# Hybrid SSD and attention block: rope's q and k blocks as two pairs in seven products, adaption rows as columns, some of down's weight sums in the z stage

## The chip, the core and the metric

The kernel runs on one core of a Trainium2 chip. A core has five engines with their own instruction streams: TensorE (PE in the profile, its weight loads PEld), VectorE (DVE), ScalarE (ACT), GpSimd (POOL) and SyncE (SP, which here only issues transfers). They meet through semaphores. Data lies in device memory, in SBUF (128 partitions) and in PSUM, where TensorE accumulates. The metric is the device time of one execution in microseconds (us), the median over runs.

## What is computed

One decoder layer over x of 1024 tokens by 1024 channels in float32. A condition c gives six rows of 1024 (shift, scale and gate for two sub-layers): "adaption". Two mixers read the same normalized input, are gated, merged and projected, and a gated convolution FFN follows.

```python
mod = silu(c) @ w_ada + b_ada
sh1, sc1, g1, sh2, sc2, g2 = split(mod, 6)
h = rms_norm(x, pre_norm1_w) * (1 + sc1) + sh1
z, xbc, dt_raw, q, k, v, gates = split(h @ w_in)
y_ssd = ssd_branch(z, xbc, dt_raw, ...)      # conv, SSD in 8 chunks of 128, norm
y_att = diff_attention_branch(q, k, v, ...)  # rope on 16 of 64 dims of each of 16 heads
merged = sigmoid(g_s) * (y_ssd @ w_ssd_o) + sigmoid(g_a) * (y_att @ w_attn_o)
x = x + g1 * rms_norm(merged @ w_out, post_norm1_w)
h2 = rms_norm(x, pre_norm2_w) * (1 + sc2) + sh2
f = (gelu(conv(h2 @ w_up)_gate) * conv(...)_val) @ w_down
x = x + g2 * rms_norm(f, post_norm2_w)
```

Rope turns r1, r2 (the first and second eight of a head's first 16 dims) into r1*cos - r2*sin and r1*sin + r2*cos.

## The kernel before

**Products.** Each float32 operand is split in a high part (`F32R`, made by ScalarE) and the rest, the low part (made by VectorE), and each product of 128x128 with 128x512 becomes three: high*high, high*low, low*high (`mm3`, `block_half`). A block of 128 output channels over all tokens is 8 x 3 products for each half of the tokens, 48 in all. Two blocks taken together as a pair, split in quarters, need seven part products of 4 x 3 in place of eight: 84 in place of 96 (the list `order`, with b11, b21, t2, t1, t3, b22, t4 for the sums of the right side and banks X, Y, Z to collect them).

**Stages**, in order: a head (norm of x, four first blocks, gates 2 and 3); the pairs; z; SSD with the v products as filler; the four rope blocks; the SSD output blocks `so`; attention with the remaining q, k and gate blocks as filler; the attention output; the mix; up in pairs; down in pairs.

**The pairs** (line 292, loop at 703). Eight pairs: four gate blocks, q and k block 2, ten xbc blocks. In product p of pair m, TensorE does 12 products, then the other engines: `x_ahead` splits the weights of three products ahead, `x_sum` makes the weight sums `sab`, ScalarE and VectorE carry the banks to `cgv`, and `post` works on the pair before (tanh for gates, convolution and silu for xbc, split and store for q and k) at the products that `steps_at` names. In pairs 1 and 2 VectorE also adds up adaption.

**Adaption** (`ada_load`, `ada_sum`, `row_load`, `ada_row`). The last four of the six rows are made from 32 tiles of 128 input channels by 1024: each is scaled by its channel's silu(c) and added to `accr` by one scalar_tensor_tensor of 128x1024 (lines 441 and 443). Fourteen fall in pairs 1 and 2, eighteen in z. Where a row is complete (z tiles 2, 7, 14, 22) TensorE sums it over the partitions by two products with `ones` (line 896), VectorE adds the bias and the norm weight on one partition (lines 897 to 901), and it is stored to `rowd`. Rows `rowd[1]` and `rowd[2]` are read back as columns `sh2c`, `a2c`; `rowd[0]` and `rowd[3]` are spread over the partitions as g1r and g2r.

**z** (loop at 906). Three thirds of the width, eight tiles of 128 tokens each, numbered nz. A tile is 24 products of 346 or 348 columns; ScalarE and VectorE make z*(1 + tanh(z/2)) in one of two tiles `ev` (lines 930, 931), which SP stores. In tiles 7 and 15 the next third's weights are split (line 95). Four banks take turns.

**SSD** (loop at 1204). 16 units (chunk, group). `chunk_in` turns x and B by transpositions into a bank px, ScalarE copies it to `xtk`, VectorE makes the masked product `cbm` and `xd` = x*dt (line 1087), GpSimd `xdd` and the skip term in y. `chunk_out` and `chunk_state` follow, between them `fill` emits v products. `down_sums` makes the four weight sums of the later down stage, 44 additions of 128x512 for 11 pairs of blocks, one at each `next(sums_dn)`, four places a unit.

**Rope and so** (loops at 1291 and 1313). q0, k0, q1, k1 hold the 16 rotated dims of all heads. `rope` scales, shuffles partitions on VectorE, multiplies on GpSimd and VectorE, adds, splits; `store_qk` stores 16 pieces of 16 rows a block. Between the blocks `turn_y` transposes the stored y, four token tiles `yr` at a time: the first half in blocks 0 and 1, then `load_y(1)`, the second half in blocks 2 and 3. `fetch_seq` and `split_seq` bring weights two to three blocks ahead. `so` then does eight blocks, both halves of each in turn, with the gate rows `gth` loaded one block ahead.

**What sets the order.** In these stages the order is written out by hand: each engine and SP's queue runs the instructions in the order of the calls (`manual_schedule`). Transfers that stand between the stages are placed by the framework. SBUF tiles of 4 KB a partition come from `Slots`, a list of 43 that is used first in, first out.

Of the kernel before, what the change touches and what calls it, by code (L numbers as in the profile page):

```python
# [14 lines left out]
ALU = mybir.AluOpType  # L15
# [15 lines left out]
NVEC = 269  # L31
# [31 lines left out]
def kernel(ctx: ExitStack, tc: tile.TileContext, a: dict, out: bass.AP, dbg=None):  # L63
# [228 lines left out]
    pairs = [("gs", 4, 5), ("gs", 6, 7), ("qk", 2, 2)] + [("xbc", b, b + 1) for b in range(2, 12, 2)]  # L292
# [25 lines left out]
    qd = [dp.tile([P, S], F32, tag=f"qd{m}", name=f"qd{m}") for m in range(NH)]  # L318
    khd = [dp.tile([64, S], F32, tag=f"khd{m}", name=f"khd{m}") for m in range(NH)]
    kld = [dp.tile([64, S], F32, tag=f"kld{m}", name=f"kld{m}") for m in range(NH)]  # L320
    acd = dp.tile([2 * NH, S], F32, tag="acd", name="acd")
    rowd = [dp.tile([1, D], F32, tag=f"rowd{i}", name=f"rowd{i}") for i in range(4)]
# [7 lines left out]
    def store_qk(kind, b, hi, lo):  # L330
        hi, lo = hi.bitcast(F32), lo.bitcast(F32)
        pieces = []
        if b < 2:
            pieces = [(8 * b + m, 0, 16 * m, 16) for m in range(8)]
        else:
            r = 0
            while r < P:
                m, d0 = divmod((b - 2) * P + r, 48)
                n = min(48 - d0, P - r)
                pieces.append((m, 16 + d0, r, n))  # L340
                r += n
        for m, d0, r, n in pieces:
            if kind == "w_q":
                SP.dma_start(qd[m][d0 : d0 + n, :], hi[r : r + n, :])
                SP.dma_start(qd[m][64 + d0 : 64 + d0 + n, :], lo[r : r + n, :])
            else:
                SP.dma_start(khd[m][d0 : d0 + n, :], hi[r : r + n, :])
                SP.dma_start(kld[m][d0 : d0 + n, :], lo[r : r + n, :])
# [24 lines left out]
    def x_load():  # L373
# [4 lines left out]
        src = {"gs": ("w_gate", "w_gate"), "xbc": ("w_xbc", "w_xbc"), "qk": ("w_q", "w_k")}[kind]["fv".index(n)]  # L378
# [45 lines left out]
    n_ada, n_ald = 0, 0  # L424
    ada_of = {}

    def ada_load():
        nonlocal n_ald
        if n_ald < 32:
            r, k = divmod(n_ald, KD)  # L430
            ada_of[n_ald] = adas[n_ald % len(adas)]
            SP.dma_start(ada_of[n_ald], a["w_ada"][k * P : (k + 1) * P, r * D : (r + 1) * D])
            n_ald += 1

    def ada_sum(load=True):
        nonlocal n_ada
        r, k = divmod(n_ada, KD)
        acc, src = accr[r % 2], ada_of.pop(n_ada)
        n_ada += 1
        if k == 0:  # L440
            V.tensor_scalar(acc, src, scl[:, 0:1], None, op0=ALU.mult)
        else:
            V.scalar_tensor_tensor(acc, src, scl[:, k : k + 1], acc, op0=ALU.mult, op1=ALU.add)
# [6 lines left out]
    u_of = {}  # L450

    def post(m, step):
        kind, *ij = pairs[m] if m >= 0 else ("xbc", 0, 1)
        n = step // 4
# [32 lines left out]
    steps_at = {"gs": {0: (0,), 1: (4,)}, "qk": {0: (0, 1), 2: (4, 5)}, "xbc": {0: (0,), 1: (1,), 2: (2,), 3: (4,), 4: (3, 5), 5: (6,), 6: (7,)}}  # L487
    part = lambda t, k: t[k // 2][:, k % 2, :]
# [13 lines left out]
    with tc.manual_schedule(engines={EN.PE, EN.DVE, EN.Activation, EN.SP}):  # L502
# [89 lines left out]
        for n, (k, half) in enumerate(units):  # L592
# [18 lines left out]
            if n == 11:  # L611
                SL.put(xT.pop(6), crow)
# [59 lines left out]
        HX["t4"] = [new_hl(f"xt4_{k}") for k in range(KH)]  # L672
# [10 lines left out]
        gate_out(pg, 0, gsd[3], vev)  # L683
        for k in range(KH):
# [5 lines left out]
        SL.put(*r22, *r11)  # L690
        evs_x = [SL.get(f"xevs{i}", F32, (P, 2, HALF)) for i in range(2)]
        cgv[0] = [SL.get(f"xc{n}0") for n in "gv"]
        SL.put(vev, *r21, *b12)
        V.tensor_copy(sel, selr)
        accr = [SL.get(f"accr{i}") for i in range(2)]
# [7 lines left out]
        for m, (kind, *_) in enumerate(pairs):  # L703
# [10 lines left out]
            for p in range(7):  # L714
# [31 lines left out]
                for st in steps_at[before].get(p, ()):  # L746
                    post(m - 1, st)
                if m in (1, 2):
                    ada_sum(n_ald < 14)
                    if m == 2 and p == 6:  # L750
                        SL.put(*adas)
                if last:
# [129 lines left out]
    brow, nrow = SL.get("brow"), SL.get("nrow")  # L882
# [1523 lines left out]
```

## Time and profile before

| | us |
|---|---|
| median of 3 runs | 1866.56 (1864.87 to 1866.98) |
| the profiled execution | 1867.69 |
| its span | 1865.8 |
| TensorE busy | 1830.3 |
| VectorE busy | 1311.8 |
| ScalarE busy | 873.2 |
| GpSimd busy | 147.9 |

Times within the profile count from the start of the span. Rows of groups name the line, engine, operation, output and inputs and their shapes, the count, the busy time and the mean of one in ns, and the idle time before them with what ended it. Rows of waits give who waited for whom, the total, the times and the longest. Rows of stretches give from:to, length, then busy time and instructions of PE, PEld, DVE, ACT and POOL, the granted clock of TensorE, the busy share of the DMA engines and GB/s. Timeline rows give start, length, engine, line and operation; equal instructions in a row are merged. Matmuls overlap, so their recorded length is longer than their pace.

### The profile page before, as it was taken

Reading aid. Unit: us, or ns where it says so; the run is one execution under the profiler, and the core shown is the slowest. Engines: PE = TensorE matmul, PEld = TensorE weight load, DVE = VectorE, ACT = ScalarE, POOL = GpSimd, SP = SyncE. Lnnn points to the kernel's source line nnn. Section 1 sums busy time; section 2 is a strip of 40 time slices with the busy share of each in tenths; the row PEclk is TensorE's granted clock in tenths of the full one; section 3 lists DMA queues with packets and bytes.
Section 4 is the critical chain, followed back from the end, with each engine's and each line's share of the span. In section 5 each row is a group of like instructions: output and inputs, shape, how many; then the busy total and the mean of one; then the engine's idle time right before and its main releaser. Section 6 shows DMA issues by size and latency. Waiting matters only on the chain.

```text
span 1865.8 us, 24318 instructions
## 1 busy us (share of the span) xinstructions
PE 1830.3 (98%) x8928; PEld 1524.9 (82%) x8928; DVE 1311.8 (70%) x1962; ACT 873.2 (47%) x1705; POOL 147.9 (8%) x137
## 2 busy tenths in 40 slices
PE   8999999998999999999999999999999999999998
PEld 6788899876788888888887888887788888888886
DVE  7887877799654257767667464487888888876545
ACT  4454532455532135565556232564545454465532
POOL 0000000165411000000000000000000000000001
PEclk9999999999999999999999999999999999999999
DMA  9564366598646746565634655122233322378744
GB/s 363 166 225 170 103 209 227 180 325 306 211 132 180 259 129 175 164 181 143 193 111 136 229 194 185 46 102 102 102 109 111 108 89 104 109 238 304 245 152 159
DMA packets 133382, 325.44 MB, mean 174 GB/s; under 512 B 17392, under 2 KB 41840, under 8 KB 133264
## 3 DMA queue, kind: packets, MB, share of 16 engines
q1 hardware_dynamic: 131952, 320.71, 52.2%
q0 software_dynamic: 1312, 3.19, 0.4%
q8 instruction: 70, 1.15, 0.3%
q14 instruction: 48, 0.39, 0.1%
HBM read 228.54 MB, written 95.31 MB: 174 GB/s over the span
## 4 chain that ended last, share of the span: by engine, by line
PE 74%; DVE 13%; ACT 6%; DMA 4%; issue 3%; POOL 0%; SPq 0%; POOLq 0%; DVEq 0%; ACTq 0%
PE upx L1822 3%; PE upx L1821 3%; PE upx L1823 3%; PE o L1513 3%; PE dx L2185 2%; PE dx L2186 2%; PE dx L2184 2%; PE dy L2184 2%; PE dy L2186 2%; PE dy L2185 2%; PE ao L118 2%; PE so L116 2%; PE so L117 2%; PE ao L117 2%; PE ao L116 2%
## 5 line engine op out<-in xcount | busy, mean ns | idle before, releaser
L1821 PE MATMUL upx<-t,wu_t 128*128 128x512 f32 x264 | 103.6, 392 | 2.3 <-ACT evs L2241 1.5
L1822 PE MATMUL upx<-t,wu_t 128*128 128x512 f32 x264 | 103.0, 390 | 0.2 <-DVE t L1939 0.2
L1823 PE MATMUL upx<-t,wu_t 128*128 128x512 f32 x264 | 102.8, 390 | 0.0
L1795 ACT ACTIVATE wu_t<-sab 128x512 fp32r<-128x512 f32 x57 | 34.1, 627 | 129.8 <-DVE sab L1812 129.8
L1501 ACT COPY aT<-at 128x512 f32<-128x512 f32 (+2 forms) x96 | 46.0, 480 | 103.0 <-PE at L1500 103.0
L95 DVE TENSOR_TENSOR g_lo<-gst,g_hi 128x1024 fp32r<-128x1024 f32 (+1 forms) x42 | 47.5, 1134 | 50.3 <-ACT g_hi L94 50.3
L1513 PEld LDWEIGHTS o<-vt,aT 128*128 128x128 f32 x576 | 74.6, 191 | 9.6 <-ACT aT L1501 5.7
L1513 PE MATMUL o<-vt,aT 128*128 128x128 f32 x576 | 81.0, 277 | 0.2
L94 ACT ACTIVATE g_hi<-gst 128x1024 fp32r<-128x1024 f32 (+1 forms) x42 | 41.4, 988 | 65.2 <-DMA gst<-gld_s 36.6
L1474 DVE TENSOR_REDUCE nmx<-sc 128x1 f32<-128x640 f32 (+3 forms) x64 | 65.6, 1024 | 2.2
L1454 PE MATMUL sc<-kst,qst 128*128 128x512 f32 (+2 forms) x192 | 63.9, 341 | 0.0
L1455 PE MATMUL sc<-klo,qst 128*128 128x512 f32 (+2 forms) x192 | 63.3, 346 | 0.0
L1821 PEld LDWEIGHTS upx<-t,wu_t 128*128 128x128 f32 x264 | 49.6, 188 | 14.6 <-ACT evs L2241 2.0
L1839 DVE SCALAR_TENSOR_TENSOR ug<-cg,vec,ug 128x1023 f32<-128x1023 f32 (+1 forms) x44 | 56.3, 1280 | 6.8 <-ACT ug L1838 5.9
L1822 PEld LDWEIGHTS upx<-t,wu_t 128*128 128x128 f32 x264 | 49.6, 188 | 10.6 <-DVE t L1939 0.5
L1799 DVE TENSOR_TENSOR wu_t<-sab,wu_t 128x512 fp32r<-128x512 f32 x57 | 39.3, 690 | 26.6 <-ACT wu_t L1795 26.6
L1823 PEld LDWEIGHTS upx<-t,wu_t 128*128 128x128 f32 x264 | 49.6, 188 | 10.3
L1839 DVE SCALAR_TENSOR_TENSOR uv<-cv,vec,uv 128x1023 f32<-128x1023 f32 (+1 forms) x44 | 56.2, 1277 | 0.9 <-ACT uv L1838 0.9
L149 POOL TENSOR_TENSOR rsf<-rsf,nhalf 128x1 f32<-128x1 f32 x8 | 5.6, 701 | 627.8 <-DVE rsf L148 625.1
L1490 DVE RECIPROCAL rsm<-ssum 128x2 f32<-128x2 f32 x64 | 10.6, 166 | 63.3 <-ACT p L1487 36.2
L1500 PE MATMUL at<-ident,p 128*128 128x128 f32 x288 | 47.8, 275 | 6.4 <-DVE p L1492 4.9
L1492 DVE SCALAR_TENSOR_TENSOR p<-p,coef,p 128x128 f32<-128x128 f32 (+3 forms) x64 | 52.4, 818 | 2.3
(550 smaller groups left out, 5921.1 us busy)
## 6 DMA issues: line engine op xcount, KB each, us to landing
adas<-in_w_ada SPq DMA_DIRECT2D x32, 512.0 KB, 5.1
wdr<-in_w_down SPq DMA_DIRECT2D x22, 512.0 KB, 6.6
wtd<-wds SPq DMA_DIRECT2D x22, 512.0 KB, 4.8
wuf<-in_w_up SPq DMA_DIRECT2D x22, 512.0 KB, 3.4
gld_s<-gsum SPq DMA_DIRECT2D x22, 512.0 KB, 2.8
gst<-gld_s SPq DMA_DIRECT2D x20, 512.0 KB, 4.4
wdt_raw<-wtd SPq DMA_DIRECT2D x20, 512.0 KB, 4.8
wuv<-in_w_up SPq DMA_DIRECT2D x19, 512.0 KB, 3.5
```

The source lines that it names most:

```text
L116: T.matmul(ps, lh, rh, start=(i == 0), stop=False)
L117: T.matmul(ps, lh, rl, start=False, stop=False)
L1454: T.matmul(sc[:, n0:n1], qs_[s][:, tsl], ks_[s][:, n0:n1], start=True, stop=False)
L1474: V.reduce_max(nmx[:, bq, s : s + 1], sc[:, :L], axis=AX.X, negate=True)
L1513: T.matmul(po_of[j, grp][:, qi, :], at[:, k, :], vt[j % 2][:, kt, :], start=(kt == 0), stop=(kt == i))
L1821: T.matmul(out_, wh, xh_, start=(k == 0 and first), stop=False, skip_group_check=not first)
L1822: T.matmul(out_, wh, xl_, start=False, stop=False, skip_group_check=not first)
L1823: T.matmul(out_, wl, xh_, start=False, stop=(k == end), skip_group_check=not first)
L1839: V.scalar_tensor_tensor(u[:, d:], c_[:, : S - d], fw[:, 2 - d : 3 - d], u[:, d:], op0=ALU.mult, op1=ALU.add)
L2184: T.matmul(o, gh[:, kk, tsl], wh, start=(k == 0 and not more), stop=False, skip_group_check=more)
L2185: T.matmul(o, gh[:, kk, tsl], wl, start=False, stop=False, skip_group_check=more)
L2186: T.matmul(o, gl[:, kk, tsl], wh, start=False, stop=(k == KF - 1), skip_group_check=more)
```

## The change

- **Rope.** q0 with k0 and q1 with k1 become pairs 3 and 4 of the pairs stage (ten pairs now). The order of the rotated dims within a block is changed, so that partners lie 64 partitions apart; two transfers within SBUF exchange the halves into `sw`, and VectorE multiplies, adds and splits in steps named by `steps_at["rope"]`, the last one in the pair after. q, and k's high and low parts, lie in device memory as one array each, so that a block of 16 dims is stored by one transfer for each part.
- **Before so.** Only w_q block 3 is left there (taken from attention's filler). Its two halves carry the first four and the next four transpositions of y; then come half 0 of so 0, four transpositions of the second half, half 0 of so 1, the other four, and then the second halves. Attention's first filler is 8 units in place of 20.
- **Adaption.** The weights lie transposed; each tile of 128 outputs by 1024 inputs is multiplied with the row `crow` and summed to one column of `adac`, the bias as start (`dot`, line 183). `ada_end`, in z tile 22, makes all columns, transposes two groups on TensorE and stores two rows; `sh2c` and `a2c` are columns of `adac`.
- **Down's sums.** Loads begin in z tile 8, and tiles 10 to 21 take one sum each; SSD units have three places in place of four.
- **SSD.** `xd` reads the bank px in place of `xtk`.
- Some tiles change places in `Slots`: `crow` is kept to the end of z, r11 is freed before the tiles of t4 are taken, b12 earlier.

```diff
-    pairs = [("gs", 4, 5), ("gs", 6, 7), ("qk", 2, 2)] + [("xbc", b, b + 1) for b in range(2, 12, 2)]
+    pairs = [("gs", 4, 5), ("gs", 6, 7), ("qk", 2, 2), ("rope", 0, 0), ("rope", 1, 1)] + [("xbc", b, b + 1) for b in range(2, 12, 2)]
...
         if b < 2:
-            pieces = [(8 * b + m, 0, 16 * m, 16) for m in range(8)]
+            for src, dst, d0 in ((hi, qd, 0), (lo, qd, 64)) if kind == "w_q" else ((hi, khd, 0), (lo, kld, 0)):
+                SP.dma_start(dst[b, d0 : d0 + 16, :, :].rearrange("d h s -> (d h) s"), src)
+            return
...
-        if k == 0:
-            V.tensor_scalar(acc, src, scl[:, 0:1], None, op0=ALU.mult)
-        else:
-            V.scalar_tensor_tensor(acc, src, scl[:, k : k + 1], acc, op0=ALU.mult, op1=ALU.add)
+        dot(adac[:, n_ada : n_ada + 1], src, crow, src, vec[:, V_BA + n_ada : V_BA + n_ada + 1])
...
+        elif kind == "rope":
+            w_, d = ("w_q", "w_k")[n], step % 5
+            sw = swt[n]
+            if d == 0:
+                SP.dma_start(sw[:64, :], c_[64:, :])
+                SP.dma_start(sw[64:, :], c_[:64, :])
+            elif d == 1:
+                V.scalar_tensor_tensor(c_, c_, qscale[w_], rop[0], op0=ALU.mult, op1=ALU.mult)
+            elif d == 2:
+                V.scalar_tensor_tensor(sw, sw, qscale[w_], rop[1], op0=ALU.mult, op1=ALU.mult)
+            elif d == 3:
+                V.tensor_tensor(c_, c_, sw, op=ALU.add)
+                A.activation(sw.bitcast(F32R), c_, AF.Copy)
+            else:
+                V.tensor_tensor(c_.bitcast(F32R), c_, sw, op=ALU.subtract)
+                store_qk(w_, b, sw, c_)
...
+    steps_at["rope"] = {0: (0,), 1: (5,), 2: (1,), 3: (2, 6), 4: (3,), 5: (7, 4), 6: (8,)}
...
+                if m > 1 and pairs[m - 2][0] == "rope" and p == 0:
+                    post(m - 2, 9)
...
-    def ada_row(r):
...
-        for half in range(2):
...
-            T.matmul(pr, ones, acc[:, hsl], start=True, stop=True)
-            V.tensor_tensor(br[:, hsl], pr[0:1, :], br[:, hsl], op=ALU.add)
...
+    def ada_end():
...
+        V.scalar_tensor_tensor(a2c, a2c, 1.0, vcol(V_PN2), op0=ALU.add, op1=ALU.mult)
+        V.scalar_tensor_tensor(gcol[:, :KD], adac[:, :KD], 0.5, vcol(V_PO1), op0=ALU.mult, op1=ALU.mult)
+        V.tensor_tensor(gcol[:, KD:], adac[:, 3 * KD :], vcol(V_PO2), op=ALU.mult)
...
+        T.transpose(pr[: 2 * KD, :P], gcol, ident)
+        V.tensor_copy(growt[: 2 * KD, :], pr[: 2 * KD, :P])
...
-                if nz in (2, 7, 14, 22):
-                    ada_row((2, 7, 14, 22).index(nz))
+                if nz == 22:
+                    ada_end()
+                if nz == 8:
...
+                    sums_dn = all_sums()
+                    down_load(0)
+                    down_load(1)
+                elif 10 <= nz < 22:
+                    next(sums_dn)
...
-        V.tensor_tensor(v3(xd[:, gs]), v3(xtk[:, gs]), bc64(dt[:, c, hs]), op=ALU.mult)
+        V.tensor_tensor(v3(xd[:, gs]), v3(px), bc64(dt[:, c, hs]), op=ALU.mult)
...
-            next(sums_dn, None)
             if u % 2 == 1:
                 chunk_norm(u // 2)
...
-    seq = [("w_q", 0), ("w_k", 0), ("w_q", 1), ("w_k", 1)] + [("w_ssd_o", j) for j in range(8)]
+    seq = [("w_q", 3)] + [("w_ssd_o", j) for j in range(8)]
...
+        for half in range(2):
+            block_half(ps[:, half, :], seq_w[0], hT, half)
+            for k in range(4 * half, 4 * half + 4):
+                turn_y(k, 0)
+            if half == 0:
+                split_seq(1)
+        load_y(1)
...
+        store_qk("w_q", 3, hi, lo)
...
+        def so_half(j, half):
+            if half == 0:
+                pso[j] = ps_mm(f"so{j}")
+                fetch_seq(j + 3)
+                SP.dma_start(gths[j % 2], gsd[j])
+            block_half(pso[j][:, half, :], seq_w[j + 1], yT, half)
+            if half == 0:
+                split_seq(j + 2)
...
+            V.scalar_tensor_tensor(mout[:, hsl], gth[:, hsl], 1.0, pso[j][:, half, :], op0=ALU.add, op1=ALU.mult)
...
+        so_half(0, 0)
+        for k in range(4):
+            turn_y(k, 1)
+        so_half(1, 0)
+        for k in range(4, 8):
+            turn_y(k, 1)
...
+        so_half(0, 1)
+        so_half(1, 1)
...
-    NFIRST, NLAST = 20, 20
+    NFIRST, NLAST = 8, 20
```

More of the change, by code (lines that the diff above doesn't have):

```diff
@@ L683 @@
         gate_out(pg, 0, gsd[3], vev)
+        SL.put(*r11)
+        HX["t4"] = [new_hl(f"xt4_{k}") for k in range(KH)]
         for k in range(KH):
@@ L959 @@
     assert n_ada == 32
-    SL.put(*ev, zraw, *cgv[1], *adas, *accr, brow, nrow)
+    SL.put(*ev, zraw, *adas, crow)
     singles.close()
@@ L1268 @@
     hi, lo = [SL.get(f"th{n}", F32R) for n in ("hi", "lo")]
-    qf = SL.get("qf")
-    sw = SL.get("sw")
-    perm = [(i + 8) % 16 + 16 * (i // 16) for i in range(32)]
     def split_seq(n):
```

179 lines of the change are left out of this document (65 added, 114 removed).

## The prediction

> **What bounds the kernel.** I read the page's busy shares first, then the busy time by stretches cut at the stage borders, then TensorE's waits.
>
> ```profile
> span 1865.8 us, 24318 instructions
> PE 1830.3 (98%) x8928; PEld 1524.9 (82%) x8928; DVE 1311.8 (70%) x1962; ACT 873.2 (47%) x1705; POOL 147.9 (8%) x137
> core 0: us, PE busy (x) PEld busy (x) DVE busy (x) ACT busy (x) POOL busy (x), PEclk, DMA share, GB/s
> 94.30:248.10 153.80, 153.04 (x674) 126.01 (x673) 128.15 (x164) 78.48 (x119) 1.18 (x2) 1.00 0.51 171
> 248.10:349.40 101.30, 99.65 (x606) 95.35 (x605) 67.48 (x109) 26.48 (x48) 4.41 (x9) 1.00 0.67 215
> 349.40:518.80 169.40, 162.65 (x842) 128.26 (x841) 143.51 (x196) 93.00 (x249) 87.50 (x63) 1.00 0.75 261
> 518.80:569.60 50.80, 50.80 (x257) 42.74 (x256) 29.81 (x36) 20.38 (x30) 11.33 (x5) 1.00 0.44 123
> 569.60:656.60 87.00, 87.00 (x385) 72.10 (x384) 26.06 (x33) 11.71 (x13) 3.43 (x1) 1.00 0.73 228
> ```
>
> The stretches are: pairs in seven products, z, SSD with v, the four rope blocks, the SSD output blocks (so). TensorE is never without work for long, at granted clock 1.00. So a product taken away counts in full, unless something then comes late, and the question is where the wait moves. The so stretch gives the pace: 384 products of 128x512 in 87.0 us, 0.2266 us each. The waits that TensorE has in these stretches:
>
> ```profile
> PE pst L1133 <- DVE tt L1116: 5.6, 4, 2.5
> PE z L117 <- DVE wz_lo L95: 1.7, 1, 1.7
> ```
>
> **1. Rope's blocks as two pairs.** Four blocks of 48 products, 192, become two pairs of 7 x 12, 168: 24 x 0.2266 = **-5.4 us**. w_q 3 only changes stage: its 48 products (10.9 us) leave attention's filler and enter before so.
>
> The pairs bring their rotation into the stage. In one pair VectorE does 7 splits, 4 sums and 3 evictions (all 128x512, 14 in all) and for rope 4 scalar_tensor_tensor and 4 additions or subtractions of 128x1024:
>
> ```profile
> L395 DVE TENSOR_TENSOR xw_t<-xsab,xw_t 128x512 fp32r<-128x512 f32 x24 | 16.6, 690 | 10.5 <-ACT xw_t L394 10.5
> L478 DVE SCALAR_TENSOR_TENSOR xbcT<-xcv,vec,xbcT 128x1023 f32<-128x1023 f32 (+2 forms) x18 | 23.0, 1279 | 1.3 <-ACT xbcT L475 1.1
> L1284 DVE TENSOR_TENSOR qf<-qf,sw 128x1024 f32<-128x1024 f32 x4 | 4.9, 1226 | 9.1 <-POOL qf L1282 9.1
> 190.00:209.00 19.00, 19.00 (x85) 15.73 (x85) 16.07 (x21) 10.17 (x15) 0.00 (x0) 1.00 0.36 112
> ```
>
> 14 x 0.69 + 4 x 1.28 + 4 x 1.23 = 19.7 us recorded, in a pair of 84 x 0.2266 = 19.0; instructions overlap by some 0.08 each, so 17.9 is needed: VectorE is 94% full, where an xbc pair shows 16.07 of 19. The lag grows through two pairs. ScalarE's copy that makes q's high half waits for VectorE's addition, and behind that copy are queued the next weight split and the copy of bank X, which product 2 of the next pair needs. Following both queues by these durations, TensorE waits 0.2 us at the second rope pair and 1.4 at the pair behind it, where ScalarE's convolution start comes on top. I take **+1.5**, bounds 0 (products are split three ahead) and 4 (the lag in every pair left). The exchange of halves is a transfer on SP's queue that is read two to three products (5.4 to 8.2 us) later. In all, 16 transfers of the rotation (8 exchanges, 8 stores) replace 64 stores on that queue. The second pair's exchange must wait until the first pair's store has read the same tile, and behind it on SP stand the next weight loads; those have four products (10.9 us) before a sum reads them. I price SP at nothing in this stage; without that cover it would be a few us, and the bound of 4 holds it.
>
> **2. Adaption rows.** The products with ones go:
>
> ```profile
> 259.54 0.33 PE L118 MATMUL z<-wz_hi,hT 128*128 128x346 f32 x1
> 259.70 1.88 PE L896 MATMUL adar<-accr,ones 128*128 128x512 f32 x4
> ...
> 261.58 0.32 PE L117 MATMUL z<-wz_lo,hT 128*128 128x346 f32 x1
> ```
>
> Without a row L117 would follow at 259.86; it comes at 261.58, so a row costs 1.72 and four cost 6.9. But a row also covered VectorE at the end of a third of z, where the next third's low weights are split:
>
> ```profile
> 280.38 2.45 DVE L95 TENSOR_TENSOR wz_lo<-wz_raw,wz_hi 128x692 fp32r<-128x692 f32 x3
> 280.43 1.88 PE L896 MATMUL adar<-accr,ones 128*128 128x512 f32 x4
> 313.32 1.27 DVE L897 TENSOR_TENSOR brow<-adar,brow 1x512 f32<-1x512 f32 x2
> 314.62 1.21 DVE L899 SCALAR_TENSOR_TENSOR brow<-brow,nrow 1x1024 f32<-1x1024 f32 x1
> 315.76 2.45 DVE L95 TENSOR_TENSOR wz_lo<-wz_raw,wz_hi 128x696 fp32r<-128x696 f32 x3
> ```
>
> At the first border the first low part is ready 0.82 after 280.38, at 281.2. Without the row TensorE wants it at 280.6: a new wait of 0.7. At the second border L897 and L899 go (2.4 us of VectorE), a down sum of 0.6 comes in, and TensorE is itself 1.72 earlier: the wait of 1.7 stays. Last, the new transposition behind tile 22 stands in TensorE's queue and waits for a VectorE chain behind that tile's own eviction:
>
> ```profile
> L930 ACT ACTIVATE ev<-z 128x330 f32<-128x330 f32 (+2 forms) x24 | 10.9, 454 | 69.2 <-PE z L118 44.7 <-DVE sm L926 24.5
> L931 DVE SCALAR_TENSOR_TENSOR ev<-ev,z 128x330 f32<-128x330 f32 (+2 forms) x24 | 12.2, 507 | 23.8 <-ACT ev L930 21.5 <-DMA zd<-ev 2.4
> L203 DVE TENSOR_TENSOR a<-a,vec 128x1 f32<-128x1 f32 x8 | 1.3, 159 | 0.3
> ```
>
> 0.45 + 0.51 + 3 x 0.16 and a transposition of 0.1 make 1.5 us; the old row found its sums long done. In all -6.9 + 0.8 + 1.5 = **-4.6**, bounds -8.6 (no wait left) and -2. The multiply-and-sum has the form of line 184, below, against the scalar_tensor_tensor of the same width (1279 above). So it is the same VectorE time, beside products; its loads keep their count and size, and the small loads of rows on POOL's queue and of two columns on SP's go at no gain, since nothing waited for them.
>
> ```profile
> L184 DVE CUSTOM_DVE_ANT_0 ada0a<-ada0a,crow,vec 128x1024 f32<-128x1024 f32 x3 | 3.8, 1277 | 0.0
> ```
>
> **3. Down's sums and SSD.** 12 of 44 sums move to z, and xd reads PSUM:
>
> ```profile
> L783 DVE TENSOR_TENSOR wds<-wdr,wds 128x512 f32<-128x512 f32 x11 | 13.4, 1219 | 0.4
> L786 DVE TENSOR_TENSOR wds<-wdr,wdr 128x512 f32<-128x512 f32 x11 | 8.7, 793 | 0.0
> L1087 DVE TENSOR_TENSOR xd<-xtk,sm 128x512 f32<-128x512 f32 x16 | 14.8, 924 | 0.0
> L1116 DVE TENSOR_TENSOR tt<-po,sm 128x512 f32<-128x512 f32 x14 | 9.5, 680 | 0.0
> ```
>
> These sums cost 0.79 to 1.22 here, about 1.0, so 12 us leave SSD. xd takes the form of tt: 16 x (0.924 - 0.680) = 3.9 us less. xd starts no earlier, since the masked product before it on VectorE still follows ScalarE. VectorE falls from 143.5 to some 127 of 169. TensorE's wait in SSD (5.6) is for tt, so for its lag; total idle is 169.4 - 162.65 = 6.75. I take **-4.5**, bounds 0 and -6.7: one of four slots per unit goes, the lag shrinks but the burst before tt stays.
>
> **4. Before so.** This order has less cover. The second half of y may load only after the first half's last transposition, and its own transpositions now come after one half block (24 x 0.2266 = 5.4 us), where before two half blocks and more lay between:
>
> ```profile
> 537.62 1.47 PE L1263 MATMUL ytr<-ident,yr 128*128 128x128 f32 x12
> L1169 SPq DMA_DIRECT2D yr<-yd x4: 319/377/1027, 538.8 to 540.8; - x4
> DMA to landing us min/median/max: 6.8/6.8/6.8
> 543.08 0.42 SPq L344 DMA_DIRECT2D qd<-thhi  x1
> gth<-gsd SPq DMA_DIRECT2D x8, 512.0 KB, 5.7
> ```
>
> The transpositions end at 539.1 (537.62 + 1.47), the fourth load is issued at 540.8 and lands 6.8 later, at 547.6: 8.5 us. So TensorE waits 8.5 - 5.4 = 3.1. Behind the loads SP holds 8 stores of w_q 3 (which wait for VectorE), one weight block and then the gate rows: issued some 9 us after those transpositions (VectorE's low half done at 5.7, then eight issues of 0.42), 5.7 to landing, so at 14.5. VectorE's first product with the gate waits for them, and the second four transpositions need the banks that VectorE frees behind it: 1.4 more. **+4.5**, bounds 1 and 9.
>
> **5. The rest.** Attention starts with 2 filler units in place of 14 (8.2 us less cover for its first loads, which are issued before so ends): +0.5, bounds 0 and 2. The transfers added to z are taken at +0.5, bounds 0 and 3 (rival C).
>
> **Sum.** -5.4 - 4.6 - 4.5 + 1.5 + 4.5 + 0.5 + 0.5 = -7.5 us. The profiled execution took 1867.7 (span 1865.8 and 1.9 around it), 1.1 above the median of 1866.6: 1860.2 for such an execution, **1859 us** for the median.
>
> **Rivals.** A: the load before so takes its upper bound, 9 us in place of 4.5. For it: SP's queue and the bank chain hold each other. Against it: the loads are first in line. 1859 + 4.5 = 1864.
> B: SSD's lag is not made by the moved sums, so that part does nothing: 1859 + 4.5 = 1863.5. For it: the sums before tt stay. Against it: the wait is for tt, which stands behind two sums in VectorE's order.
> C, the slower side: z runs out of transfers.
>
> ```profile
> 286.00:346.00 60.00, 58.35 (x359) 56.00 (x358) 38.59 (x68) 12.43 (x25) 2.42 (x5) 1.00 0.71 225
> 410.00:425.00 15.00, 14.89 (x79) 11.52 (x78) 14.48 (x19) 8.21 (x21) 8.88 (x7) 1.00 1.00 366
> ```
>
> 60 us move 13.5 MB; five loads of 1 MB and three stores of 1 MB, less the three loads of 0.5 MB already there, add 6.9: 20.4 MB want 340 GB/s. SSD shows that 366 is possible. If z gets 275, its transfers need 74 us; 14 late, in front of VectorE's in-order queue and of SSD's first weights: 1859 + 14 = 1873. It decides above some 8 us of lateness, at 300 GB/s. [...]
> D: the wait before so throttles TensorE.
>
> ```profile
> 20.00:24.00 4.00, 3.33 (x11) 1.72 (x10) 2.73 (x8) 1.75 (x5) 1.02 (x1) 0.72 1.03 422
> 432.00:436.00 4.00, 1.58 (x7) 0.94 (x6) 3.96 (x6) 0.59 (x1) 0.30 (x1) 1.00 0.94 359
> ```
>
> In the head, after gaps, the granted clock fell to 0.72 over 4 us, a loss of 0.28 x 4 = 1.1 us; 2.4 us without a product at 432 left it at 1.00. With 3.1 in one piece it may fall: 1860. [...]
> E: the new waits of 1, 2 and 4 are half what I take, and SSD gives all of its 6.7: about 1853.
>
> **Chances.** Forecast (1855 to 1862.5) 0.54; A 0.11; B 0.08; C 0.11; D 0.07; E 0.09. About 0.2% (3.7 us) is what a measurement of this kernel can tell from no change. Faster: the forecast, D and E, 0.70; within it A and B, 0.19; slower C, 0.11. The range 1851 to 1868 leaves out C and the edge of E.
>
> **What would show it.** The pairs stretch has 840 products and about 192 us; rows of line 896 are gone; TensorE waits for the transposition behind z's tile 22 and for the low weights at the first border; SSD is shorter by 4 to 5 us with "pst from tt" small; before so TensorE waits for the load of y some 3 us; one product stage of 48 and 384 of so with 64 transpositions take about 105 us and those waits. It is wrong if the pairs wait in every pair, if z's low weights or v's come late for transfers, or if y's load lands 12 us after its transpositions.

## The result and the profile after

The changed kernel takes 1909.62 us (median of 4 runs, 1906.27 to 1914.37) against 1866.57 for the kernel before: a ratio of 1.0234, 95% interval 1.0211 to 1.0258. It is slower by 43 us, where 7.5 us of gain were forecast. Its profiled execution took 1906.27, with a span of 1904.5.

The stretches of the changed kernel, cut at the same stage borders as in the prediction (from:to, length, busy time of PE, PEld, DVE, ACT and POOL with instructions, granted clock, DMA share, GB/s): pairs, z, SSD, then w_q 3 with so, and then, counted again from the same start, everything up to the first block of the attention output.

```profile
94.10:296.50 202.40, 192.58 (x841) 157.12 (x840) 164.76 (x222) 94.94 (x145) 0.00 (x0) 1.00 0.53 177
296.50:402.50 106.00, 96.30 (x598) 94.95 (x597) 67.13 (x131) 25.35 (x46) 1.04 (x1) 0.97 0.75 258
402.50:568.40 165.90, 161.73 (x834) 127.62 (x833) 122.29 (x182) 92.97 (x248) 79.60 (x62) 1.00 0.63 223
568.40:708.80 140.40, 115.17 (x507) 93.93 (x506) 37.47 (x53) 24.12 (x38) 0.92 (x2) 0.93 0.47 159
568.40:1080.20 511.80, 480.86 (x2626) 404.63 (x2624) 292.74 (x578) 244.06 (x624) 17.05 (x18) 0.98 0.53 158
```

The last line answers to this stretch of the kernel before:

```profile
518.80:1042.00 523.20, 516.08 (x2818) 436.51 (x2817) 316.03 (x603) 253.91 (x637) 31.27 (x22) 1.00 0.56 166
```

Four blocks of 48 products have left that stretch, 192 x 0.2266 = 43.5 us. So 479.7 was to be had, and with the forecast waits of 5 us 484.7; it took 511.8. That is the largest miss, 27.1 us. TensorE is idle for 511.80 - 480.86 = 31 us there, and the granted clock fell to 0.98 in the mean, 0.93 up to 708.80. The second is z, 106.0 where 96.7 + 0.5 was forecast. The third is the pairs: two more pairs, 168 products or 38.1 us, should have made 153.8 into 191.9 and a wait of 1.5; they take 202.4. SSD is 3.5 us shorter, about as forecast. Behind attention both kernels take the same, 823.8 and 824.3.

TensorE's waits in the changed kernel show the three places:

```profile
PE so L117 <- DVE mout L1319: 21.3, 5, 8.4
PE xx L416 <- ACT xevs L741: 5.9, 3, 3.0
PE z L117 <- ACT wz_hi L95: 5.4, 1, 5.4
PE ytr L1275 <- DMA yr<-yd: 3.9, 3, 2.0
PE xx L416 <- DVE xcv L755: 2.8, 3, 2.0
PE z L118 <- DVE wz_lo L96: 2.3, 2, 1.5
PE adat L913 <- DVE gcol L911: 2.0, 1, 2.0
```

### so: the gate rows

In the groups of VectorE, the product with the gate idles for a transfer (first row). In the kernel before (second row) it had 50.9 us of idle time, all for TensorE's products:

```profile
L1319 DVE SCALAR_TENSOR_TENSOR mout<-gth,so 128x512 f32<-128x512 f32 x16 | 11.0, 687 | 92.0 <-DMA gth<-gsd 46.9 <-PE so L119 45.1
L1329 DVE SCALAR_TENSOR_TENSOR mout<-gth,so 128x512 f32<-128x512 f32 x16 | 10.3, 684 | 50.9 <-PE so L118 50.9
```

The timeline of one border between blocks, first SP's queue, then VectorE and TensorE:

```profile
643.57 0.32 SPq L1321 DMA_DIRECT2D msd<-mout  x1
643.94 0.42 SPq L1258 DMA_DIRECT2D qst<-qd  x1
644.41 1.44 SPq L1261 DMA_DIRECT2D kst<-khd  x2
645.89 1.23 SPq L1261 DMA_DIRECT2D klo<-kld  x2
647.22 0.53 SPq L1199 DMA_DIRECT2D w_ssd_o_raw<-in_w_ssd_o  x1
647.80 0.43 SPq L1313 DMA_DIRECT2D gth<-gsd  x1
655.51 0.69 DVE L1319 SCALAR_TENSOR_TENSOR mout<-gth,so 128x512 f32<-128x512 f32 x1 [10.84 <-DMA gth<-gsd]
656.25 0.79 PE L117 MATMUL so<-yT,w_ssd_o_hi 128*128 128x512 f32 x1 [8.00 <-DVE mout L1319]
```

The store of a block's result waits until the block is done. Behind it on SP's queue stand attention's first loads (behind blocks 3 and 4), a weight block, and then the gate row that the running block needs at its middle. It is issued at 647.80 and there at 655.5; TensorE's second half waits 8.0 us for VectorE's product with it. Without attention's loads in front (blocks 2 and 3) the same wait is 2.5 and 2.3 us. A block now loads its own gate row, where the kernel before loaded the next block's. There attention's first loads also stood behind the gate row on the queue, and not ahead of it.

### z: a store behind loads

```profile
337.70 2.81 SPq L800 DMA_DIRECT2D wdr<-in_w_down  x4
340.60 2.10 SPq L358 DMA_DIRECT2D wz_raw<-in_w_zdt  x3
342.80 0.42 SPq L358 DMA_DIRECT2D zraw<-in_w_zdt  x1
343.48 0.79 SPq L946 DMA_DIRECT2D zd<-ev  x1
352.01 0.52 DVE L945 SCALAR_TENSOR_TENSOR ev<-ev,z 128x346 f32<-128x346 f32 x1 [7.61 <-DMA zd<-ev]
362.54 0.31 ACT L877 ACTIVATE sm<-sm 128x128 f32<-128x128 f32 x1 [6.03 <-DVE sm L876]
363.59 2.11 ACT L95 ACTIVATE wz_hi<-wz_raw 128x696 fp32r<-128x696 f32 x3
364.41 0.66 PE L117 MATMUL z<-wz_hi,hT 128*128 128x348 f32 x1 [5.39 <-ACT wz_hi L95]
```

Down's four loads of 512 KB and the four loads of the next third's weights are issued just ahead of a store of z. Only two tiles `ev` take turns, so VectorE waits 7.61 us until that store has read its tile. All that stands behind on VectorE and ScalarE is late by it: ScalarE waits for `sm`, and behind that stand the weight splits of the last third. TensorE waits 5.39 us for them and starts again at half its pace: up to 369.94 the granted clock is 0.50 and the products start 0.29 us apart, from 370.20 on it is 1.00 and they start 0.16 apart. While the burst runs, the DMA engines are busy all the time (0.96 and 1.03 in the column before the last), though z as a whole shows 0.75:

```profile
340.00:345.00 5.00, 5.00 (x34) 5.00 (x33) 4.23 (x12) 0.69 (x3) 0.00 (x0) 1.00 0.96 351
345.00:350.00 5.00, 5.00 (x33) 5.00 (x32) 0.00 (x0) 0.46 (x1) 0.00 (x0) 1.00 1.03 372
```

### Pairs: the exchange

```profile
201.03 0.33 SPq L335 DMA_DIRECT2D kld<-xcv  x1
201.63 1.20 SPq L377 DMA_DIRECT2D xwv<-in_w_xbc  x1
202.94 0.47 SPq L462 DMA_DIRECT2D sw<-xcv  x1
209.71 1.23 DVE L465 SCALAR_TENSOR_TENSOR xcv<-xcv,ropc 128x1024 f32<-128x1024 f32 x1 [2.64 <-DMA sw<-xcv]
213.33 0.50 PE L416 MATMUL xx<-xt,xw_t 128*128 128x512 f32 x1 [1.96 <-DVE xcv L755]
222.99 1.24 ACT L489 ACTIVATE xbcT<-xcg,vec 128x1024 f32<-128x1024 f32 x1
224.13 0.57 ACT L741 COPY xevs<-xx 128x512 f32<-128x512 f32 x1
224.76 0.50 PE L416 MATMUL xx<-xt,xw_t 128*128 128x512 f32 x1 [2.98 <-ACT xevs L741]
```

The second rope pair's exchange for k stands on SP behind the first pair's last store, which waits for VectorE, and a weight load. Its first half is issued at 202.94, and at 209.71 VectorE, which multiplies in place, has waited 2.64 us for it. The lag comes out at TensorE as 1.96 us in that pair and 2.98 in the next.

### The profile page after: what moved, and what is told of

The parts are those of the page before. It is cut to its first block, busy times and chain, and to the rows that moved or that the text cites. A ratio compares the mean times of both kernels' runs of the same rounds, so it can differ in the third digit from the quotient of the medians.

```text
span 1904.5 us, 24191 instructions
## 1 busy us (share of the span) xinstructions
PE 1831.0 (96%) x8889; PEld 1522.7 (80%) x8889; DVE 1303.8 (68%) x2004; ACT 878.7 (46%) x1717; POOL 121.3 (6%) x122
## 4 chain that ended last, share of the span: by engine, by line
PE 67%; DVE 14%; DMA 9%; ACT 5%; issue 2%; SPq 1%; POOL 0%; DVEq 0%; POOLq 0%; ACTq 0%
PE upx L1822 3%; PE upx L1823 3%; PE upx L1824 3%; PE o L1518 3%; PE at L1505 2%; PE dx L2186 2%; PE ao L118 2%; PE ao L119 2%; PE ao L117 2%; PE dx L2187 2%; PE upy L1822 2%; PE dx L2185 1%; PE upy L1823 1%; PE upy L1824 1%; PE sc L1460 1%
## 5 line engine op out<-in xcount | busy, mean ns | idle before, releaser
L1518 PEld LDWEIGHTS o<-vt,aT 128*128 128x128 f32 x576 | 74.8, 191 | 10.1 <-ACT aT L1506 6.0
L1319 DVE SCALAR_TENSOR_TENSOR mout<-gth,so 128x512 f32<-128x512 f32 x16 | 11.0, 687 | 92.0 <-DMA gth<-gsd 46.9
L117 PE MATMUL so<-yT,w_ssd_o_hi 128*128 128x512 f32 x128 | 52.9, 413 | 21.3 <-DVE mout L1319 21.3
L416 PE MATMUL xx<-xt,xw_t 128*128 128x512 f32 x120 | 47.6, 396 | 9.8 <-ACT xevs L741 5.9
```

The lines of the kernel that those rows point to most:

```text
L117: T.matmul(ps, lh, rh, start=(i == 0), stop=False)
L416: T.matmul(o, wh, xh_, start=(k == 0 and first), stop=False, skip_group_check=not first)
L1518: T.matmul(po_of[j, grp][:, qi, :], at[:, k, :], vt[j % 2][:, kt, :], start=(kt == 0), stop=(kt == i))
```

## The experiments

All are the changed kernel with one edit, unless the text says otherwise. "Stage" means here the stretch from the last v product to the attention output (511.8 us in the changed kernel).

### Gate rows one block ahead

```diff
+        for n in range(2):
+            SP.dma_start(gths[n], gsd[n])            # ahead of the w_q 3 block
...
-                SP.dma_start(gths[j % 2], gsd[j])
+                if 2 <= j < 7:
+                    SP.dma_start(gths[(j + 1) % 2], gsd[j + 1])
...
         so_half(0, 1)
+        SP.dma_start(gths[0], gsd[2])
         so_half(1, 1)
```

> The changed kernel, with the gate rows of a block loaded one block ahead again (rows 0 and 1 ahead of the second half of y, row j+1 at the start of block j), as the kernel before did. Theory G, that the late gate rows carry the loss in so: VectorE's idle time for the gate rows falls from 46.9 us to under 10, TensorE's wait for the product with the gate from 21.3 to under 5, and the time by 18 to 24 us, to 1886 to 1892. Rival Y, that the reload of y and the lower clock behind it carry the loss: the gate rows only take a wait that another one replaces, and the time falls by under 8 us, to 1902 or more.

Measured: 1883.11 us, 26.5 less than the changed kernel (1.0089 of before, 1.0074 to 1.0105). VectorE's group and TensorE's waits between 610 and 670 us of this kernel:

```profile
L1322 DVE SCALAR_TENSOR_TENSOR mout<-gth,so 128x512 f32<-128x512 f32 x16 | 11.0, 687 | 62.3 <-PE so L119 62.3
PE so L117 <- DVE mout L1322: 3.9, 5, 0.8
```

No idle time for gate rows is left, and the stage takes 489.1. Theory G holds, and gives some 2 us more than it asked for; rival Y is out as the main cause. Two things remain: five waits of 0.78, and the reload of y.

### Both products with the gate behind the second half

```diff
-            V.scalar_tensor_tensor(mout[:, hsl], gth[:, hsl], 1.0, pso[j][:, half, :], op0=ALU.add, op1=ALU.mult)
             if half == 1:
+                for h_ in range(2):
+                    hsl = slice(h_ * HALF, (h_ + 1) * HALF)
+                    V.scalar_tensor_tensor(mout[:, hsl], gth[:, hsl], 1.0, pso[j][:, h_, :], op0=ALU.add, op1=ALU.mult)
                 SP.dma_start(msd[j], mout)
```

This is on top of the gate rows one block ahead.

> The changed kernel with the gate rows one block ahead and both products with the gate of a block behind the block's second half, as the kernel before had them, where the changed kernel puts the first product between the halves. With the gate rows alone five or six blocks show a wait of TensorE of 0.78 us at the second half for the first half's product (3.9 us in all; six stretches of 10 us show 9.22 busy). If the order makes it (the second half writes the same tile that the product reads): these waits go, and the time falls by 4 to 5 us, to 1878 to 1879. If VectorE is late for another reason, the wait moves to the next block's first half: within 1.5 us of 1883.

Measured: 1878.75, 4.4 us less than with the gate rows alone; the stage 483.7 in place of 489.1, and the row "so from mout" is gone from TensorE's waits. The changed kernel asks VectorE to read one half of a two-half PSUM tile while TensorE is to write the other; the program makes TensorE wait until that read is done (0.78 us a time: the 0.69 of the product and its way). That wait was hidden under the late gate rows.

### A second set of tiles for y

```diff
+        ysets.append([SL.get(f"yr{i}") for i in range(4, 8)])
+        load_y(1)                                     # at the start of the w_q 3 block
...
-        load_y(1)
```

Two kernels have it: the changed kernel with this edit alone, and the one with the gate rows one block ahead.

> The changed kernel, with a second set of four tiles for y, so that the second half of y is loaded at the start of the w_q 3 block and not behind the first half's last transposition; the gate rows still come when the changed kernel loads them. If the waits add up: TensorE's gap of some 5.4 us at the second half's transpositions goes and the clock behind it stays at 1.00, so the time falls by 6 to 8 us, to 1902 to 1904. If the gate rows are the later of the two anyway, they take the wait's place: under 3 us.

Measured: 1909.13, the same as the changed kernel (1909.62). TensorE no longer waits for y's load, but 2.8 us for VectorE at the same transpositions, and its wait for the gate product is 22.9 us in place of 21.3: the gate rows were the later of the two.

> The changed kernel with the gate rows one block ahead and a second set of tiles for y. With the gate rows alone it took 1883.1, and from the end of v to the first output block of attention 489.1 us, with 3.17 us of 588 to 593 without a product and the granted clock at 0.92 and 0.74 there (4.5 and some 1.7 us lost). If the reload of y and the clock behind it are hidden by the second set: 5 to 7 us less, 1876 to 1878, and the clock 1.00 throughout so. If something else holds the second half's transpositions (the banks, VectorE): less than 2 us.

Measured: 1880.23, 2.9 us less than with the gate rows alone (1883.11), where 5 to 7 were expected; the stage falls from 489.1 to 483.7, by 5.4. The granted clock is 1.00 in the whole stage. The stage shows the expected size; the whole time shows less. In its profiled execution z and SSD, which this edit does not touch, are longer (z 106.6 in place of 105.8, SSD 167.0 in place of 166.2).

### Down's sums in SSD again

```diff
-                if nz == 8:
-                    ...
-                    down_load(0)
-                    down_load(1)
-                elif 10 <= nz < 22:
-                    next(sums_dn)
...
             run_bg(1)
+            next(sums_dn, None)                       # fourth place of an SSD unit
```

> The changed kernel, with all of down's weight sums in SSD again and none in z. Theory Z, that the loads of down's weights stand ahead of z's stores: VectorE's wait for the stores of z (14.3 us) falls to about 2.4 as before, TensorE's wait for the high weights (5.4) goes, z takes 97 to 99 us in place of 105.7; SSD takes 0 to 4 us more, since 12 sums of about 1 us return to a VectorE with slack. Time 4 to 8 us lower. Rival: the multiply-and-sum columns and the new transposition make z's waits; then z stays over 103 us, and the time is the same or up to 4 us higher.

Measured: 1898.87, 10.7 us less. z takes 95.9 in place of 106.0, and SSD 167.2 in place of 165.9. Theory Z holds, its size was set too low. It also prices two parts of the change apart: the adaption columns bring z from 101.3 to 95.9, 5.4 us; the moved sums gain 1.3 in SSD and cost 10.1 in z.

### Four tiles for z's stores

```diff
-    ev = [SL.get(f"ev{i}", F32, (P, 2, HALF)) for i in range(2)]
+    ev = [SL.get(f"ev{i}", F32, (P, 2, HALF)) for i in range(4)]
```

> The changed kernel with four tiles for what z stores in place of two; down's sums and their loads stay in z, and nothing else moves. Theory Z, that only the turn of two store tiles passes the late transfer on to VectorE, ScalarE and TensorE: VectorE's wait for z's stores (14.3 us) falls under 3, TensorE's wait for the high weights (5.4) under 1, z falls from 106.0 to 97 to 99 us, and the time by 6 to 9 us. Rival C, that z has more to move than its transfers manage: the late transfer then shows at the weights of z or at the adaption's loads, z stays over 102 us, and the time falls by less than 4.

Measured: 1904.49, 5.1 us less. z itself follows theory Z. This kernel's stretches z and the first 23 us of SSD, TensorE's wait at the start of SSD, and the issue of v's first weights on SP's queue:

```profile
295.50:391.90 96.40, 94.16 (x597) 92.94 (x595) 65.88 (x129) 24.18 (x44) 1.04 (x1) 1.00 0.78 273
391.90:415.00 23.10, 16.94 (x80) 13.49 (x80) 13.94 (x25) 14.24 (x36) 4.28 (x4) 0.85 0.52 179
PE v L1056 <- ACT wv_hi L1034: 6.2, 1, 6.2
393.45 1.45 SPq L1025 DMA_DIRECT2D wv_raw<-in_w_v  x3
```

z falls to 96.4, so the two store tiles were what passed the lateness on. But SSD rises from 165.9 to 171.9: now v's first weights are late, a wait of 6.2 us, with a clock of 0.85 over the 23 us. The eight loads of v's weights take 5.0 us in the median from issue to landing (5.7 in the changed kernel). But the first of them are issued only behind the last store of z, at 393.45, where the changed kernel issues the first one at 377.38, 25 us before z ends. So this wait comes from the time of their issue and not from slow transfers. Why this kernel places them so late, and whether z would still be short with them further ahead, no run shows.

### The exchange on POOL's queue

```diff
-                SP.dma_start(sw[:64, :], c_[64:, :])
-                SP.dma_start(sw[64:, :], c_[:64, :])
+                G.dma_start(sw[:64, :], c_[64:, :])
+                G.dma_start(sw[64:, :], c_[:64, :])
...
-            sw = swt[n]
+            sw = swt[2 * b + n]
```

> The changed kernel, with the exchange of halves of the two rope pairs issued on POOL's queue, which is empty in that stage, and into tiles of its own for each pair. Theory S, that the exchange comes late on SP's queue: VectorE's wait of 2.6 us for the exchange goes, TensorE's waits at the second rope pair and the two behind it (2.5 + 3.0 + 0.6 us) fall to 1.5 to 3, and the time falls by 3 to 4.5 us. Rival V, that VectorE is simply full there (94% by my own sum): the waits move by less than 1 us and the time by less than 1.5.

Measured: 1905.87, 3.7 us less; the pairs take 199.6 in place of 202.4, and VectorE no longer waits for the exchange. The pairs stretch of kernels in which nothing of it was changed went from 201.1 to 204.0, so a gain of 3 is about what can be told here. Theory S is supported, and half of the waits stay. The edit gives the exchange another queue and tiles of its own at once; which of the two frees it, this run does not tell.

### A tile that is still being stored

```diff
-        SL.put(vev, *r21)
+        SL.put(*r21, vev)
```

> The changed kernel with one line of the list of free tiles turned round, so that the first convolution's output in the pairs stage doesn't get the tile of which the last gate block is still being stored. TensorE's wait in the first pair falls from 2.4 us to 0.5 as in the kernel before; time 2 us lower, which the runs can hardly tell. If it stays 2.4, ScalarE waits for something else there.

TensorE's waits in the first pair (94 to 113 us) of this kernel; in the changed kernel the same row has 2.4, since ScalarE's convolution start waits 1.8 us for a store of the last gate block to leave its tile:

```profile
PE xx L416 <- ACT xevs L741: 0.5, 1, 0.5
```

The pairs take 200.8 in place of 202.4, the time is 1905.24; the difference of 4.4 to 1909.62 is more than the row explains, and within the spread of the changed kernel's own runs.

### All of it together

Gate rows ahead, products with the gate behind the second half, a second set for y, down's sums in SSD, the exchange on POOL's queue, the tile handed out last.

> The changed kernel with all of it together: gate rows one block ahead, both products with the gate behind the second half, a second set of tiles for y, down's sums in SSD again, the exchange of halves on POOL's queue with tiles of its own per pair, and the slot of the last gate tile of the first stage handed out last (that one should take the wait of 2.4 us at the first pair). If the effects add up: 1909.6 - 26.5 - 10.7 - 3.7 - 4.5 - 6 - 2 = 1856, range 1853 to 1860, faster than the kernel before (1867). If the rope pairs keep a lag of VectorE's own, or a new wait comes up: 1861 to 1867.

Measured: 1858.27 (1857.15 to 1859.49), 0.9955 of before (0.9940 to 0.9970). The single gains add up to 26.5 + 4.4 + 2.9 + 10.7 + 3.7 + 4.4 = 52.6, which would give 1857.0. The changed kernel's loss is accounted for as a whole; the smaller gains in this sum are within the spread of the runs, so it does not confirm them one by one. Its stretches are pairs, z, SSD and the stage:

```profile
93.80:291.80 198.00, 193.29 (x842) 158.27 (x841) 164.82 (x222) 94.77 (x145) 4.27 (x8) 0.99 0.55 182
291.80:387.70 95.90, 94.20 (x598) 93.23 (x597) 61.25 (x121) 26.98 (x50) 2.08 (x2) 1.00 0.68 226
387.70:554.90 167.20, 162.85 (x833) 128.23 (x833) 132.70 (x193) 90.97 (x245) 81.47 (x61) 0.99 0.72 257
554.90:1033.00 478.10, 472.45 (x2625) 400.18 (x2624) 292.49 (x578) 243.41 (x624) 17.03 (x18) 1.00 0.57 169
```

### Columns and xd alone

The kernel before with the adaption columns (and the places of tiles that they need) and `xd` from PSUM; rope, the order before so and down's sums are as before.

```diff
-                if nz in (0, 4, 8, 16):
-                    row_load((0, 4, 8, 16).index(nz))
-                if nz in (2, 7, 14, 22):
-                    ada_row((2, 7, 14, 22).index(nz))
+                if nz == 22:
+                    ada_end()
...
-        V.tensor_tensor(v3(xd[:, gs]), v3(xtk[:, gs]), bc64(dt[:, c, hs]), op=ALU.mult)
+        V.tensor_tensor(v3(xd[:, gs]), v3(px), bc64(dt[:, c, hs]), op=ALU.mult)
```

> The kernel before with two parts of the change alone: the four adaption rows as multiply-and-sum columns, and xd from PSUM. Rope stays four blocks behind v, down's sums stay in SSD, the order before so is the old one. If these two parts carry all that the repaired change gains: z 96 to 97 us in place of 101.4, SSD 167 in place of 169.3, time 1858 to 1860, no slower than the repaired change (1858.3). If the rope pairs are worth their 5.4 us of products: this kernel is about 4 us slower than the repaired one, 1862.

Measured: 1858.27 (1857.65 to 1859.26), 0.9956 of before (0.9944 to 0.9969): the same as the repaired change. Its pairs take 153.8, z 95.8, SSD 166.5 and the stage 523.2. So in the repaired change rope's pairs and their new order gain nothing that these runs can tell: 198.0 + 478.1 = 676.1 against 153.8 + 523.2 = 677.0. The 24 saved products (5.4 us) are spent on the waits in the pairs, 198.0 - 153.8 - 38.1 = 6.1 us; the stage itself is back at what it should take.

### What holds the rope pairs

Two edits of the repaired change (1858.27), each with one step of the rotation on GpSimd, which computes nothing else there.

```diff
-                V.scalar_tensor_tensor(c_, c_, qscale[w_], rop[0], op0=ALU.mult, op1=ALU.mult)
+                G.tensor_tensor(c_, c_, rop[0], op=ALU.mult)      # the scale goes to the copy and the subtraction
```

> The repaired change (1858.3 us) with one of the two multiplications per block of the rotation on GpSimd in place of VectorE (3.4 us each there in the kernel before, 1.2 on VectorE), and the scale of q in the copy and the subtraction. It takes 2 x 1.2 us off a VectorE that is full in the rope pairs. If VectorE's own length makes the waits left at the pair behind the rope pairs (2.5 + 0.5 us, clock 0.91): they fall under 1 and the time by 2 to 4 us, 1854.5 to 1856.5. If the chain of steps makes them (the exchange, then the multiplications, the addition, ScalarE's copy in front of the next weight split): GpSimd's longer multiplication makes the chain longer, the waits stay or grow, 1858 to 1861.

Measured: 1860.88, 0.9968 of before (0.9955 to 0.9980); the pairs 200.6 in place of 198.0. Taking 2.4 us a pair off VectorE does not help, and the chain gets longer: each multiplication takes 2.4 to 2.9 us on GpSimd. Both were changed at once, so this run does not show what a shorter VectorE alone would bring.

```diff
-                A.activation(sw.bitcast(F32R), c_, AF.Copy)
+                G.tensor_copy(sw.bitcast(F32R), c_)
```

> The repaired change (1858.3 us) with the copy that makes the rotated blocks' high half on GpSimd in place of ScalarE. The traces so far show ScalarE with that copy at the head of its queue waiting 1.9 to 5.0 us for VectorE's addition, and behind it the next weight split, the copy of a bank and the convolution's start; the copy of the bank at 218.98 is what TensorE waits 2.5 us for. If ScalarE's queue behind this copy makes the waits: they fall from 2.5 + 0.5 to under 1 and the time by 2 to 3.5 us, 1854.5 to 1856.5. If VectorE's lag itself makes them (it is busy without a gap from 202.8 to 212.6 in the second rope pair's turn), or its subtraction now waits for the longer copy on GpSimd: the waits stay and the time is 1857.5 or more.

Measured: 1855.76 (1854.11 to 1859.20), 0.9944 of before (0.9930 to 0.9958), with pairs of 196.2. The copies take 1.0 to 1.4 us on GpSimd, and TensorE's largest wait in the pair behind is now one for VectorE:

```profile
L470 POOL CAST sw<-xcv 128x1024 fp32r<-128x1024 f32 x2 | 2.9, 1438 | 9.1 <-DVE xcv L469 9.1
L470 POOL CAST sw<-xcg 128x1024 fp32r<-128x1024 f32 x2 | 2.1, 1042 | 21.9 <-DVE xcg L469 21.9
PE xx L416 <- DVE xcv L755: 1.8, 1, 1.8
```

The wait of 2.5 us for ScalarE's copy of the bank is gone; so ScalarE's queue behind the copy made it. Of VectorE's own lag 1.8 us stays. This is the fastest kernel of the study, 11 us below the kernel before; against the repaired change and against columns with xd alone (both 1858.27) its median is 2.5 us lower, but the intervals of the ratios overlap.

## Why the prediction was wrong, step by step

| step | forecast, us | measured, us | from |
|---|---|---|---|
| 1, products saved | -5.4 | -5.4 | 840 products in the pairs and 192 fewer in the stage, at the same pace |
| 1, waits in the pairs | +1.5 (0 to 4) | +10.5 | 202.4 - 153.8 - 38.1 |
| 2, adaption columns | -4.6 (-8.6 to -2) | -5.4 | z 101.3 to 95.9 with the sums in SSD |
| 3, SSD | -4.5 (-6.7 to 0) | -3.5 | 169.4 to 165.9 |
| 4 and attention's start | +5.0 (1 to 11) | +32.1 | 511.8 - (523.2 - 43.5) |
| 5, transfers in z | +0.5 (0 to 3) | +10.1 | 106.0 - 95.9 |
| sum | -7.5 | +38.4 | the span: 1904.5 - 1865.8 = 38.7 |

**The step that failed is part 4, "Before so": "+4.5, bounds 1 and 9".** It priced the load of y and the gate row of the first block, and then stopped. That each later block loads its own gate row, at its own start, behind the store of the block before, was in the diff and not in the sum. The prediction had the row that tells the price, 5.7 us to landing for such a load, against 5.4 us of products that it must fit into, with 0.9 to 4.2 us of queue in front (630.09 to 630.94 at block 2's end, 643.57 to 647.80 at block 3's, where the row then took 7.7 to land). It is a wait in blocks 2 to 5, and 22.7 us of the stage, 26.5 of the time. The same step missed the wait of 0.78 us at each second half, 5.4 us in the stage; and of the reload itself it took 3.1 where the reload's removal saves 5.4 with the clock. Rival A, the load before so at 9 us, had the right stage but not the place: that load cost 5.4, and most of the loss came from the gate rows of later blocks.

**Part 5 took +0.5 for z's transfers; they cost 10.1.** The bandwidth sum of rival C was sound in its terms, and C was given a chance of 0.11 with 14 us. But z as a whole did not run out of bandwidth: 258 GB/s were moved, and 294 in the 60 us from 334, where C reckoned with 340. The price came from one burst of loads that filled the DMA engines for 10 us (shares of 0.96 and 1.03 from 340 to 350), ahead of one store, with two tiles taking turns behind it; with four tiles z takes 96.4 with the same loads in it. The average over 60 us could not show that. Nor are the 366 GB/s of SSD, from which rival C argued, the most that these traces show: the kernel before moved 413 from 15 to 35 us.

**Part 1's waits were +1.5 and are +10.5.** The place was right, the second rope pair and the one behind it, and so was the head of ScalarE's queue. Three terms were off. "I price SP at nothing in this stage" failed: the exchange stood behind the store that was named there. The wait at the pair behind was 2.98 and not 1.4. And the new turn of tiles, which put a convolution's output on a tile still being stored, was not looked at (2.4 us at the first pair).

**Parts 2 and 3 came out within their bounds.** Part 2 added 0.8 us for the low weights and 1.5 at the transposition. With down's sums in SSD the transposition waits 0.6, and the low weights 1.1, less than the 1.7 before; in the changed kernel, where z is late, they are 2.0 and 2.3. The cut between z and SSD has also moved a little: SSD's first transpositions, 0.7 us (349.52 to 350.21 in the kernel before), now run ahead of z's end, so z gained 6.1 and SSD 2.8. In SSD TensorE's wait for `tt` fell from 5.6 to 1.3, but a new wait of 2.2 us for v's first weights took part of that back. Rival B, no gain in SSD, is out: xd alone brings SSD to 166.5 to 167.2 with the wait for `tt` still 4.0 to 4.3, and the moved sums bring the last 1.3.

**Rival D, the clock.** It was expected at most for one gap. The changed kernel shows a granted clock of 0.50 at the reload of y (592 to 596), of 0.50 in z behind the wait of 5.4 us (366 to 369.94), and of 0.50 and 0.53 behind the waits of 8.0 and 8.4 us for a gate row (656 to 660 and 677 to 681). Around the two waits of 2.5 and 2.3 us it is 1.00 (620 to 628 and 634 to 640). Around the reload:

```profile
588.00:592.00 4.00, 0.88 (x4) 0.28 (x3) 0.00 (x0) 0.00 (x0) 0.00 (x0) 1.00 0.96 339
592.00:596.00 4.00, 3.22 (x15) 2.93 (x15) 0.00 (x0) 1.90 (x3) 0.00 (x0) 0.50 0.76 251
596.00:600.00 4.00, 4.00 (x14) 3.21 (x13) 0.00 (x0) 1.79 (x3) 0.00 (x0) 0.65 0.98 344
```

The second quad of transpositions starts at 588.27 and the next block's products at 595.95; with y loaded early the same 16 transpositions take 1.7 us. The granted clock is 0.50 from the first steady work at 593.26 to 598.65, 5.4 us. No single gap ahead of it was over 2.0 us (2.0, 1.2 and 0.7, with lone transpositions between them), where one gap of 2.48 us in the kernel before (up to 436.06) left the clock at 1.00 from 436 to 440. From 588.54 to 592.08 TensorE did one transposition of 0.33 us.

## What to carry to other kernels

When a loop is rewritten, look at every load in it and ask in which turn it was issued and in which it is used: a load that moves from one turn ahead into its own turn costs, in each turn, what its issue and landing take beyond the work that covers them (here 2.3 and 2.5 us), and more wherever something else is put ahead of it on the same queue (here 8.0 and 8.4). A stage with spare bandwidth on average (z, a DMA share of 0.75) can still have no room for a burst (0.96 and 1.03) ahead of a store whose tile is needed two steps later (a wait of 7.6 us). And when products are saved by moving work into a stage where another engine is then full (VectorE, 9.70 of 10 us from 198 to 208 in the fastest kernel), the saving is to be compared with the waits that it makes there; here 5.4 us of products bought 4.3 to 6.1 us of waits even after repair.

## What the runs showed of the hardware that was not expected

- A store of z issued directly behind eight loads held its tile until 8.5 us after its issue (343.48 to 352.01); over the whole changed kernel the 22 loads of down of 512 KB take 6.3 us in the median from issue to landing.
- The granted clock was 0.50 from 592 to 596, behind 4 us with 0.88 us of work in four instructions (588 to 592). In the kernel before, 1.58 us of products in 4 us (432 to 436) had left it at 1.00 (436 to 440).
- A copy of 128x1024 to fp32r took 1.0 to 1.4 us on GpSimd, near ScalarE's 1.06, where a multiplication of two operands of that size took 2.4 to 2.9 on GpSimd (3.4 in the kernel before) and 1.2 on VectorE.
